# First stage of a hybrid mixer: queries and keys/values projected together, tile by tile

## The chip, the cores and the metric

The kernel runs on one core of a Trainium2 chip. The metric is the device time of one execution in microseconds, the median of the runs. A core has five engines with instruction streams of their own: TensorE (PE; PEld are its weight loads), VectorE (DVE), ScalarE (ACT), GpSimd (POOL) and SyncE (SP), which here only issues DMAs. ScalarE issues some DMAs too, in the same stream as its arithmetic. Each stream runs in order; semaphores tie them together.

## The reference, cut to what matters

The input x has 1024 tokens of 1024 features. It is layer-normed once, then passes through two layers. A layer projects all tokens to 3992 columns, feeds four groups of heads (A: banded attention, B: a chunked recurrence, C: a gated recurrence, D: attention over compressed, selected and recent keys), projects their outputs back and norms the sum.

```python
h = layer_norm(x, ln0_g, ln0_b)
for l in range(DEPTH):                                  # 2
    y = hybrid_mixer(h, w_in[l], b_in[l], ...)          # A, B, C, D from h @ w_in[l] + b_in[l]
    h = layer_norm(DN_ALPHA * h + y, ln_g[l], ln_b[l])
```

For group D, the columns `dq` (256) are queries, which are rotated by position; `dkv` (276) holds two keys, which are rotated too, two values, and the gates of D and B; `dx` (128) is compressed over windows of 32 tokens by a small two-layer network into some 63 keys and values. All are sums over the 1024 features of h.

## The kernel before

Tokens are worked on in halves of 512, that is four tiles of 128. A stage is one half in one layer, so there are four stages; stage 0 is the first half in layer 0. In each stage the groups come in the order D, C, A, B. A group first projects, then mixes; while one group mixes, tile by tile, the program already writes the projections of the next one in between, so that TensorE has matmuls to lie beside the softmax work.

Numbers are float32 in two parts: a weight or activation is rounded to the matmul's format (`hi`) and the rest (`lo`) is kept beside it. A product is three matmuls (hi hi, hi lo, lo hi). So each weight piece that comes from memory (`load_piece`, lines 270 to 280) costs a DMA on SyncE's queue into one of two raw buffers, a cast on ScalarE (L276) and a subtraction on GpSimd (L277), and then lies in one of six split buffers (tag `W`). `load_in` brings a chunk of columns as four pieces of two feature blocks each.

In stage 0, `bring(t)` (L542) norms a tile of x in place (`norm`, lines 188 to 213: statistics on VectorE, Ln and Exp on ScalarE, four short VectorE steps, then two passes over 1024 columns, L210 subtract mean and times gain, L211 times deviation and plus bias). `to_feature` (L258) then transposes it on TensorE, in two groups of four, with a cast (L266) and a subtraction (L267) per group. `proj_tok` (L287) projects tokens: per tile 24 matmuls, three for each of eight feature blocks. For `dq` its result gets its bias (L520) and is rotated on GpSimd in five steps (`rope`, L327). `proj_feat` (L305) projects with the features in the rows, 24 matmuls of 512 columns per 128 columns.

Group D in stage 0 goes: `dq` with `bring` for the four tiles, constants (`load_consts`: masks and tables, loaded and cast on GpSimd, L252), `dx`, its compression (lines 586 to 612), `dkv` with key rotation and transposes, then the mixing, whose first step is `front(0)`; its projection `dz` (48 matmuls of 512 columns) is written after that, but may run earlier. The one-hot rows (L554 to 556) that mark key blocks are written under the keys in stages 0 and 2, and are read in stages 1 and 3.

PSUM for projections and transposes is two banks (pool `pj`). The pool with tag `P` has six buffers of 1024 columns, used for gain and bias, one-hot rows, constants on their way, the compression weights, and later for scores.

The order within each engine's stream is not that of the code alone. A planner takes the instructions by readiness in a time model, earlier code first, and writes the streams; it also ties each DMA issue to an earlier one where too many would be open.

Of the kernel before, what the change touches and what calls it, by code (L numbers as in the profile page):

```python
# [10 lines left out]
F32 = mybir.dt.float32  # L11
F32R = mybir.dt.float32r
# [3 lines left out]
OP = mybir.AluOpType  # L16
# [3 lines left out]
T, D, DEPTH = 1024, 1024, 2  # L20
NT = T // 128
TH = T // 2
NTH = NT // 2
# [131 lines left out]
def tile_hybrid(ctx, tc, I, out, dbg=None, depth=DEPTH):  # L155
# [3 lines left out]
    def f(ap):  # L159
        return ap.bitcast(F32)  # L160
# [12 lines left out]
    def cload(name, shape, q=SY):  # L173
        t_ = const.tile(shape, F32, name=name + "_sb")
        q.dma_start(t_, I[name])
        return t_

    def row_bc(src):
        return bass.AP(tensor=src.tensor, offset=src.offset, ap=[[0, 128], [1, src.shape[-1]]])
# [2 lines left out]
    acc = fix.tile([128, NTH, D], F32, tag="acc", name="acc")  # L182
    SY.dma_start(acc[:, 0, :], I['x'][0:128, :])
    ident = cload('ident', [128, 128])
    S.preload_act_table_set("natural_log_exp_and_others")


    def norm(x_t, gb, spread=False, dst=None):
        st = sm.tile([128, 2, 6], F32, tag="st", name="st", bufs=2)
        for j in range(2):  # L190
            V.bn_stats(out=st[:, j, :], in_=x_t[:, j * 512:(j + 1) * 512])
        mv = sm.tile([128, 2], F32, tag="mv", name="mv", bufs=2)
        V.bn_aggr(out=mv, in_=st)
        ve = sm.tile([128, 4], F32, tag="ve", name="ve", bufs=2)
        V.tensor_scalar(ve[:, 0:1], mv[:, 1:2], LN_EPS, None, op0=OP.add)
        S.activation(out=ve[:, 1:2], in_=ve[:, 0:1], func=AF.Ln)
        S.activation(out=ve[:, 2:3], in_=ve[:, 1:2], func=AF.Exp, scale=-0.5)
        V.tensor_tensor(ve[:, 1:2], ve[:, 2:3], ve[:, 2:3], op=OP.mult)
        V.tensor_tensor(ve[:, 1:2], ve[:, 1:2], ve[:, 0:1], op=OP.mult)
        V.tensor_scalar(ve[:, 1:2], ve[:, 1:2], -0.5, 1.5, op0=OP.mult, op1=OP.add)  # L200
        V.tensor_tensor(ve[:, 3:4], ve[:, 1:2], ve[:, 2:3], op=OP.mult)
        if spread:
            V.scalar_tensor_tensor(ve[:, 0:1], mv[:, 0:1], -1.0, ve[:, 3:4], op0=OP.mult, op1=OP.mult)
            S.activation(out=x_t, in_=x_t, func=AF.Identity, scale=ve[:, 3:4], bias=ve[:, 0:1])
            V.tensor_tensor(x_t, x_t, gb[0], op=OP.mult)
            G.tensor_tensor(x_t, x_t, gb[1], op=OP.add)
            return
        for j in range(2 if dst is not None else 1):
            c_ = slice(j * 512, (j + 1) * 512) if dst is not None else slice(0, D)
            V.scalar_tensor_tensor(x_t[:, c_], x_t[:, c_], mv[:, 0:1], gb[0][:, c_], op0=OP.subtract, op1=OP.mult)  # L210
            V.scalar_tensor_tensor(x_t[:, c_], x_t[:, c_], ve[:, 3:4], gb[1][:, c_], op0=OP.mult, op1=OP.add)  # L211
            if dst is not None:
                (SY if j else S).dma_start(dst[:, c_], x_t[:, c_])

    def load_gb(g, b, tag=None):
        if tag is not None:
            gb2 = mp.tile([128, 2, D], F32, tag=tag, name="gb2")
            gb = [gb2[:, 0, :], gb2[:, 1, :]]
        else:
            gb = [mp.tile([128, D], F32, tag="P", name="gb", bufs=PB) for _ in range(2)]  # L220
        SY.dma_start(gb[0], row_bc(g))
        SY.dma_start(gb[1], row_bc(b))
        return gb

    gb0 = load_gb(I['ln0_g'], I['ln0_b'])
    for t in range(1, NTH):
        S.dma_start(acc[:, t, :], I['x'][t * 128:(t + 1) * 128, :])
    cos = cload('cos', [128, NT, 32], S)
# [16 lines left out]
    def load_consts():  # L245

        for name, dst in (('masks', masks), ('cmask', cmask), ('lvm', lvm), ('sel', sel)):
            d2 = dst.rearrange("p a b -> p (a b)") if len(dst.shape) == 3 else dst
            n = d2.shape[1]
            m_ = mp.tile([128, 1024], F32, tag="P", name="m_", bufs=PB)  # L250
            SY.dma_start(m_[:, :n], I[name] if len(I[name].shape) == 2 else I[name].rearrange("p a b -> p (a b)"))
            G.tensor_copy(d2, m_[:, :n])  # L252
        for name, dst in (('rowok', rowok), ('rope_e', rope_e), ('impk', impk), ('rowsel', rowsel)):
            SY.dma_start(dst, I[name])
# [32 lines left out]
    def proj_tok(l, ch, evac, before=None):  # L287
        n = len(CHUNKS[ch])
        W = load_in(l, ch)
        bias = wp.tile([128, 276], F32, tag="bias", name="bias", bufs=1)  # L290
        SY.dma_start(bias[:, :n], row_bc(I['b_row'][l, CH_OFF[ch]:CH_OFF[ch] + n]))
        for t in range(NTH):
            if before is not None:
                before(t)
            ps = pj.tile([128, 512], F32, tag="pj", name="ps_p")
            for k in range(8):
                a = hT['hi'][:, k, t * 128:(t + 1) * 128]
                b = hT['lo'][:, k, t * 128:(t + 1) * 128]
                hi, lo = W[k // 2][0][:, k % 2, :], W[k // 2][1][:, k % 2, :]
                PE.matmul(ps[:, :n], a, hi, start=(k == 0), stop=False)  # L300
                PE.matmul(ps[:, :n], a, lo, start=False, stop=False)  # L301
                PE.matmul(ps[:, :n], b, hi, start=False, stop=(k == 7))  # L302
            evac(t, ps[:, :n], bias)

    def proj_feat(l, ch, evac):  # L305
        n = len(CHUNKS[ch])
# [148 lines left out]
    def groups(stage):  # L455
# [61 lines left out]
        def ev_q(dst):  # L517
            def ev(t, ps, bias):
                qt = sm.tile([128, 4, 64], F32, tag="qt", name="qt")
                V.tensor_tensor(qt, ps.rearrange("p (h d) -> p h d", h=4), bias[:, :256].rearrange("p (h d) -> p h d", h=4),  # L520
                                op=OP.add)
                rope(dst[:, t, :].rearrange("p (h z d) -> p h z d", h=4, z=2), qt, 4, cos[:, T0 + t, :], sin[:, T0 + t, :],
                     twice=True)
            return ev

        def ev_kv(dst, Vt, extra=None, rest=None, T1=T0):
            def ev(t, ps, bias):
                kt = sm.tile([128, 2, 64], F32, tag="qt", name="kt")
                V.tensor_tensor(kt.rearrange("p a b -> p (a b)"), ps[:, 0:128], bias[:, 0:128], op=OP.add)
                V.tensor_tensor(Vt[:, T1 + t].rearrange("p a b -> p (a b)"), ps[:, 128:256], bias[:, 128:256], op=OP.add)  # L530
                if rest is not None:
                    V.tensor_tensor(rest[:, t, :], ps[:, 256:276], bias[:, 256:276], op=OP.add)
                kr = sm.tile([128, 2, 64], F32, tag="kr", name="kr")
                rope(kr, kt, 2, cos[:, T0 + t, :], sin[:, T0 + t, :])
                c_ = slice((T1 + t) * 128, (T1 + t + 1) * 128)
                stack_k(kr, dst[:, 0:2, c_], 128, 128, extra=None if extra is None else extra[0:64, c_])
            return ev

        def group_D():
            hT['hi'] = fix.tile([128, 8, TH], F32R, tag="hThi", name="hT_hi")  # L540
            hT['lo'] = fix.tile([128, 8, TH], F32R, tag="hTlo", name="hT_lo")
            def bring(t):  # L542
                if stage == 0:
                    h_t = acc[:, t, :]
                    norm(h_t, gb0)
                else:
                    h_t = mp.tile([128, D], F32, tag="P", name="h_t", bufs=PB)
                    SY.dma_start(h_t, hd[hf][t])
                to_feature(h_t, t)
            if hf == 0:  # L550
                lay['Vd'] = mp.tile([128, NT, 2, 64], F32, tag="Vd", name="Vd")
                lay['KD'] = mp.tile([128, 3, T], F32R, tag="KD", name="KD")
                for j in range(2):
                    oh = mp.tile([16, 512], F32, tag="P", name="oh", bufs=PB)  # L554
                    SY.dma_start(oh, I['onehot'][:, 512 * j:512 * j + 512])
                    G.tensor_copy(lay['KD'][64:80, 2, 512 * j:512 * j + 512], oh)
                lay['vc'] = sm.tile([64, 64], F32, tag="vc", name="vc")
                G.memset(lay['vc'], 0.0)
                lay['Kc'] = sm.tile([128, 1, 64], F32R, tag="Kc", name="Kc")
                lay['xtail'] = sm.tile([128, 16], F32, tag="xtail", name="xtail")  # L560
            Vd, KD, vc, Kc, xtail = (lay[k] for k in ('Vd', 'KD', 'vc', 'Kc', 'xtail'))
            qd = mp.tile([128, NTH, 512], F32, tag="q", name="qd")
            proj_tok(l, 'dq', ev_q(qd), bring)
            if stage == 0:
                load_consts()
            yield

            XT = mp.tile([128, 2, 544], F32, tag="ca", name="XT")
# [42 lines left out]
            rope(kc[:, 1:2, :], kc[:, 0:1, :], 1, rope_e[:, hf, 0:32], rope_e[:, hf, 32:64], P=32)  # L611
            stack_k(kc[:, 1:2, :], Kc[:, :, 32 * hf:32 * hf + 32], 32, 32)

            proj_tok(l, 'dkv', ev_kv(KD, Vd, KD[:, 2, :], gi))
            gs = sm.tile([128, NTH, NH, 3], F32, tag="gs", name="gs")
            gsv = gs.rearrange("p t a b -> p t (a b)")
            S.activation(out=gsv, in_=gi[:, :, 0:12], func=AF.Exp, scale=-1.0)
# [620 lines left out]
```

## Time and profile before

| | |
|---|---|
| three runs | 1589.19, 1591.62, 1594.03 us, median 1591.62 |
| profiled execution | 1595.7 us, span 1593.9 us |
| TensorE busy (share of the span) | 1471.4 us (92%) |
| weight loads | 1184.5 us (74%) |
| VectorE | 1054.0 us (66%) |
| GpSimd | 854.2 us (54%) |
| ScalarE | 791.5 us (50%) |
| mean granted clock of TensorE | 0.973 |

Times in rows are microseconds from the first instruction of the span; a row of a timeline gives the start and then the duration. Engine names with a small q (SPq, ACTq) are the issue of DMAs. An arrow in brackets names what ended the idle time in front of an instruction. Matmuls are pipelined, so the spacing of their starts, not their duration, is what each adds.

### The profile page before, as it was taken

The page shows a single profiled execution, that of the slowest core. Times are in us where ns is not written, and L with a number is a line of the kernel's source. Part 1 is how long each engine was busy: PE and PEld are TensorE (multiplying, and loading weights), DVE is VectorE, ACT ScalarE, POOL GpSimd, SP SyncE. Part 2 cuts the span into 40 slices and gives each one's busy share as a digit, 9 for nine tenths or more (in the row PEclk, how much of TensorE's full clock was granted, in tenths as well). Part 3 has the DMA queues.
Part 4 walks back from the last instruction along what each step waited for, and adds up shares of the span by engine and source line. Part 5 has one row for each costly group of instructions (what it writes and reads, how often), then busy time and mean ns, then how long its engine had stood idle before and what let it go on. Part 6 is the DMA issues. An engine that isn't in the chain of part 4 may idle for free.

```text
span 1593.9 us, 29097 instructions
## 1 busy us (share of the span) xinstructions
PE 1471.4 (92%) x10674; PEld 1184.5 (74%) x10674; DVE 1054.0 (66%) x2494; ACT 791.5 (50%) x1865; POOL 854.2 (54%) x1182
## 2 busy tenths in 40 slices
PE   3899999989979998999998999999997999899995
PEld 3787688768867766887886877887886876588684
DVE  6347755795597788348549568359449778844767
ACT  2357535444356765345535564445534576534551
POOL 3733685556653308844576348844575330784443
PEclk9999999999989999999999999999998999999997
DMA  5221123441352100224234311224125210032311
GB/s 189 74 76 53 28 57 98 148 147 53 110 164 57 53 1 15 74 70 148 67 87 149 96 53 28 74 70 150 51 82 173 76 54 1 2 78 63 106 53 53
DMA packets 64894, 126.93 MB, mean 80 GB/s; under 512 B 10256, under 2 KB 16176, under 8 KB 64752
## 3 DMA queue, kind: packets, MB, share of 16 engines
q1 hardware_dynamic: 63888, 122.99, 26.6%
q10 hardware_dynamic: 864, 2.10, 0.4%
q8 instruction: 84, 1.38, 0.4%
q14 instruction: 58, 0.48, 0.1%
HBM read 114.57 MB, written 10.49 MB: 78 GB/s over the span
## 4 chain that ended last, share of the span: by engine, by line
PE 56%; DVE 17%; POOL 13%; DMA 5%; issue 5%; ACT 3%; SPq 0%; DVEq 0%; POOLq 0%; ACTq 0%
PE ps_f L315 6%; PE ps_f L317 6%; PE ps_f L316 6%; PE ps_pt L442 4%; PE O L449 4%; PE ps_p L300 3%; DMA w_raw<-in_w_in 3%; PE ps_p L301 3%; PE ps_p L302 3%; POOL w_split L277 3%; PE S_ps L388 2%; PE ps_o L491 2%; PE ps_o L493 2%; DVE QK L970 2%; PE ps_o L492 2%
## 5 line engine op out<-in xcount | busy, mean ns | idle before, releaser
L277 POOL TENSOR_TENSOR w_split<-w_raw,w_split 128x512 fp32r<-128x512 f32 (+2 forms) x320 | 416.5, 1309 | 379.5 <-ACT w_split L276 356.3
L276 ACT CAST w_split<-w_raw 128x512 fp32r<-128x512 f32 (+2 forms) x320 | 194.5, 610 | 246.1 <-DMA w_raw<-in_w_in 136.3
L315 PE MATMUL ps_f<-hT_hi,w_split 128*128 128x512 f32 x608 | 244.9, 403 | 0.0
L316 PE MATMUL ps_f<-hT_lo,w_split 128*128 128x512 f32 x608 | 242.6, 399 | 0.0
L317 PE MATMUL ps_f<-hT_hi,w_split 128*128 128x512 f32 x608 | 241.6, 399 | 0.0
L300 PE MATMUL ps_p<-w_split,hT_hi 128*128 128x256 f32 (+1 forms) x768 | 227.4, 299 | 12.3 <-DVE hT_lo L267 8.6
L301 PE MATMUL ps_p<-w_split,hT_hi 128*128 128x256 f32 (+1 forms) x768 | 222.9, 291 | 0.3 <-POOL w_split L277 0.3
L302 PE MATMUL ps_p<-w_split,hT_lo 128*128 128x256 f32 (+1 forms) x768 | 222.1, 290 | 0.0
L407 ACT ACTIVATE P<-S_ps,stt 128x256 f32<-128x256 f32 (+3 forms) x256 | 133.3, 528 | 69.1 <-DVE stt L402 42.5
L300 PEld LDWEIGHTS ps_p<-w_split,hT_hi 128*128 128x128 f32 x768 | 150.3, 196 | 17.3 <-DVE hT_lo L267 10.3
L301 PEld LDWEIGHTS ps_p<-w_split,hT_hi 128*128 128x128 f32 x768 | 150.2, 196 | 3.8 <-issue 2.3
L302 PEld LDWEIGHTS ps_p<-w_split,hT_lo 128*128 128x128 f32 x768 | 149.9, 195 | 1.8 <-issue 1.2
L315 PEld LDWEIGHTS ps_f<-hT_hi,w_split 128*128 128x128 f32 x608 | 114.8, 189 | 26.8 <-issue 2.9
L317 PEld LDWEIGHTS ps_f<-hT_hi,w_split 128*128 128x128 f32 x608 | 114.7, 189 | 26.6 <-issue 0.8
L316 PEld LDWEIGHTS ps_f<-hT_lo,w_split 128*128 128x128 f32 x608 | 114.9, 189 | 23.9 <-issue 0.8
L402 DVE TENSOR_REDUCE stt<-S_ps 128x1 f32<-128x384 f32 (+3 forms) x182 | 110.0, 624 | 32.3 <-PE S_ps L400 11.1
L491 PE MATMUL ps_o<-w_split,Y 128*128 128x512 f32 x256 | 111.3, 435 | 10.7 <-DVE acc L498 6.5
L442 PE MATMUL ps_pt<-ident_sb,P 128*128 128x128 f32 x648 | 104.3, 289 | 8.8 <-DVE P L432 8.2
L493 PE MATMUL ps_o<-w_split,Y 128*128 128x512 f32 x256 | 104.6, 417 | 4.3 <-POOL Y L477 4.1
L442 PEld LDWEIGHTS ps_pt<-ident_sb,P 128*128 128x128 f32 x648 | 73.8, 145 | 46.3 <-issue 38.1
L492 PE MATMUL ps_o<-w_split,Y 128*128 128x512 f32 x256 | 103.7, 405 | 0.0
L449 PE MATMUL O<-PT,Vd 128*64 128x256 f32 x528 | 84.9, 411 | 6.1 <-DVE PT L447 6.0
(359 smaller groups left out, 3172.8 us busy)
## 6 DMA issues: line engine op xcount, KB each, us to landing
w_raw<-in_w_in SPq DMA_DIRECT2D x224, 256.0 KB, 2.7
w_raw<-in_w_out SPq DMA_DIRECT2D x64, 256.0 KB, 2.7
w_raw<-in_w_in SPq DMA_DIRECT2D x16, 276.0 KB, 2.8
w<-in_w SPq DMA_DIRECT2D x8, 512.0 KB, 5.5
hs<-acc SPq DMA_DIRECT2D x8, 512.0 KB, 2.6
h_t<-hs SPq DMA_DIRECT2D x8, 512.0 KB, 4.3
acc<-hs SPq DMA_DIRECT2D x8, 512.0 KB, 4.0
out<-acc SPq DMA_DIRECT2D x7, 512.0 KB, 2.7
```

The lines of the kernel that those rows point to most:

```text
L276: S.copy(out=hi, in_=raw_)
L277: G.tensor_tensor(lo, raw_, f(hi), op=OP.subtract)
L300: PE.matmul(ps[:, :n], a, hi, start=(k == 0), stop=False)
L301: PE.matmul(ps[:, :n], a, lo, start=False, stop=False)
L302: PE.matmul(ps[:, :n], b, hi, start=False, stop=(k == 7))
L315: PE.matmul(ps, a, x1, start=(k == 0), stop=False)
L316: PE.matmul(ps, a, x2, start=False, stop=False)
L317: PE.matmul(ps, b, x1, start=False, stop=(k == 7))
L442: PE.transpose(ps[:, h, :], P[c][h // 2][:, h % 2, kb * 128 - a:kb * 128 - a + 128], ident)
L449: PE.matmul(O[64 * g:64 * g + 64, :], Vt(k0 + kb, g), PT[:, 2 * g:2 * g + 2, :].rearrange("p a b -> p (a b)"), start=(first and kb == 0), ...
L491: PE.matmul(ps, a, hi, start=(k == 0), stop=False)
L493: PE.matmul(ps, b, hi, start=False, stop=(k == 1))
```

## The change

In stage 0 alone, `dq` and `dkv` are projected together. A new function `proj_first` takes each tile through `bring`, then through the 24 matmuls of `dq` and the 24 of `dkv`. The raw weights of `dq` are requested near the top, on SyncE's queue, into two buffers of tag `P`; their split form lies in the buffers `KQ` and `Y`, which other groups use later. Gain and bias of the first norm move to ScalarE's queue, ahead of the x tiles 1 to 3. The first tile's two passes are cut into halves of 512 columns. The one-hot rows are written after `dkv`, in stages 0 and 2, and the constants after `proj_first`. The arithmetic is the same.

```diff
-    def norm(x_t, gb, spread=False, dst=None):
+    def norm(x_t, gb, spread=False, dst=None, halves=False):
...
-        for j in range(2 if dst is not None else 1):
-            c_ = slice(j * 512, (j + 1) * 512) if dst is not None else slice(0, D)
+        halves = halves or dst is not None
+        for j in range(2 if halves else 1):
+            c_ = slice(j * 512, (j + 1) * 512) if halves else slice(0, D)
...
-        SY.dma_start(gb[0], row_bc(g))
-        SY.dma_start(gb[1], row_bc(b))
+        q.dma_start(gb[0], row_bc(g))
+        q.dma_start(gb[1], row_bc(b))
...
-    gb0 = load_gb(I['ln0_g'], I['ln0_b'])
+    gb0 = load_gb(I['ln0_g'], I['ln0_b'], q=S)
+    for j in range(2):
+        first_raw.append(mp.tile([128, 2, 512], F32, tag="P", name="w_raw0", bufs=PB))
+        for z in range(2):
+            o_ = 8 * CH_OFF['dq'] + (2 * j + z) * 512
+            SY.dma_start(first_raw[j][:, z, :], I['w_in'][0, :, o_:o_ + 512])
...
+    def proj_first(bring, ev_a, ev_b):
+        W = [[], load_in(0, 'dkv')]
+        for j, tag in enumerate(('KQ', 'Y')):
+            w = mp.tile([128, 2, 2, 512], F32R, tag=tag, name="w_first")
+            for z in range(2):
+                S.copy(out=w[:, z, 0], in_=first_raw[j][:, z, :])
+                G.tensor_tensor(w[:, z, 1], first_raw[j][:, z, :], f(w[:, z, 0]), op=OP.subtract)
+                W[0].append([w[:, z, v].rearrange("p (k n) -> p k n", k=2) for v in range(2)])
...
+        for t in range(NTH):
+            bring(t)
+            for W_, n, bias, ev in ((W[0], 256, ba, ev_a), (W[1], 276, bb, ev_b)):
+                ps = pj.tile([128, 512], F32, tag="pj", name="ps_p")
+                for k in range(8):
...
+                    PE.matmul(ps[:, :n], a, hi, start=(k == 0), stop=False)
+                    PE.matmul(ps[:, :n], a, lo, start=False, stop=False)
+                    PE.matmul(ps[:, :n], b, hi, start=False, stop=(k == 7))
+                ev(t, ps[:, :n], bias)
...
-                    norm(h_t, gb0)
+                    norm(h_t, gb0, halves=(t == 0))
...
+            def block_rows():
                 for j in range(2):
                     oh = mp.tile([16, 512], F32, tag="P", name="oh", bufs=PB)
...
-            proj_tok(l, 'dq', ev_q(qd), bring)
             if stage == 0:
+                proj_first(bring, ev_q(qd), ev_kv(KD, Vd, KD[:, 2, :], gi))
                 load_consts()
+            else:
+                proj_tok(l, 'dq', ev_q(qd), bring)
...
-            proj_tok(l, 'dkv', ev_kv(KD, Vd, KD[:, 2, :], gi))
+            if stage > 0:
+                proj_tok(l, 'dkv', ev_kv(KD, Vd, KD[:, 2, :], gi))
+            if hf == 0:
+                block_rows()
```

## Rows read from the trace of the kernel before

**Rows 1.** Stretches: engines' busy us (instructions), TensorE's granted clock, DMA share, GB/s.
```profile
0.00:18.10 18.10, 0.01 (x1) 0.01 (x1) 12.58 (x32) 3.27 (x7) 5.88 (x15) 1.00 0.81 265
18.10:38.70 20.60, 13.03 (x57) 11.94 (x58) 11.54 (x20) 4.82 (x12) 8.89 (x8) 1.00 0.43 133
38.70:50.10 11.40, 9.25 (x73) 8.41 (x73) 3.95 (x7) 3.16 (x6) 10.15 (x17) 1.00 0.05 14
50.10:75.50 25.40, 22.25 (x196) 19.82 (x195) 6.60 (x19) 8.18 (x17) 18.21 (x34) 1.00 0.33 94
...
95.00:1593.90 1498.90, 1409.53 (x10270) 1129.82 (x10268) 1013.07 (x2405) 762.90 (x1803) 799.24 (x1096) 0.97 0.26 77
```

**Rows 2.** Timeline of VectorE, the first norm: start, duration, instruction.
```profile
5.60 1.29 DVE L191 BATCH_NORM_STATS2 st<-acc 128x6 f32<-128x512 f32 x2 [4.64 <-DMA acc<-in_x]
...
15.80 4.45 DVE L211 SCALAR_TENSOR_TENSOR acc<-acc,ve,gb 128x1024 f32<-128x1024 f32 x2
```

**Rows 3.** Timeline of TensorE, 18 to 56 us.
```profile
18.09 1.97 PE L262 MATMUL ps_t<-ident_sb,acc 128*128 128x128 f32 x8 [18.09 <-DVE acc L211]
...
22.97 0.58 PE L300 MATMUL ps_p<-w_split,hT_hi 128*128 128x256 f32 x1 [2.92 <-DVE hT_lo L267]
...
41.83 0.66 PE L262 MATMUL ps_t<-ident_sb,acc 128*128 128x128 f32 x4 [1.40 <-DVE hT_lo L267]
42.25 0.36 PE L300 MATMUL ps_p<-w_split,hT_hi 128*128 128x256 f32 x1
...
45.18 1.39 PE L262 MATMUL ps_t<-ident_sb,acc 128*128 128x128 f32 x8
...
55.70 0.29 PE L300 MATMUL ps_p<-w_split,hT_hi 128*128 128x276 f32 x1
```

**Rows 4.** Timeline of ScalarE and its DMA issues, up to 29 us.
```profile
0.77 1.35 ACTq L227 DMA_DIRECT2D acc<-in_x  x3
...
5.82 0.33 ACTq L175 DMA_DIRECT2D sin_sb<-in_sin  x1
8.36 0.20 ACT L196 ACTIVATE ve<-ve 128x1 f32<-128x1 f32 x1 [6.34 <-DVE ve L195]
...
28.34 0.62 ACT L276 CAST w_split<-w_raw 128x512 fp32r<-128x512 f32 x1 [3.97 <-DMA w_raw<-in_w_in]
```

**Rows 5.** Raw weight pieces issued before 30 us: from issue to landing.
```profile
DMA to landing us min/median/max: 3.1/4.2/6.2
```

**Rows 6.** Stretches around the hole at 88.2 us, columns as in the first group.
```profile
88.20:90.20 2.00, 0.00 (x0) 0.00 (x0) 0.75 (x1) 1.15 (x2) 1.14 (x1) 0.95 0.48 131
90.20:93.40 3.20, 3.17 (x15) 3.18 (x16) 1.65 (x3) 2.94 (x7) 1.54 (x2) 0.50 0.32 82
```

**Rows 7.** The x tiles 1 to 3 (line 227): from issue to landing.
```profile
DMA to landing us min/median/max: 5.0/7.2/10.0
```

**Rows 8.** Gain and bias of the first norm: from issue to landing.
```profile
DMA to landing us min/median/max: 7.4/8.9/10.4
```

**Rows 9.** Groups by line and shape on GpSimd, 0 to 95 us: busy us, mean ns.
```profile
L277 POOL TENSOR_TENSOR w_split<-w_raw,w_split 128x512 fp32r<-128x512 f32 x14 | 18.8, 1355 | 14.4 <-ACT w_split L276 14.4
L277 POOL TENSOR_TENSOR w_split<-w_raw,w_split 128x552 fp32r<-128x552 f32 x4 | 5.5, 1380 | 1.9 <-ACT w_split L276 1.8
```

**Rows 10.** Timeline of GpSimd: a constant's cast; first and last rotation step of a tile.
```profile
19.12 1.50 POOL L252 CAST masks_r<-m__407 128x384 fp32r<-128x384 f32 x1
...
46.55 0.73 POOL L331 TENSOR_TENSOR rp<-qt,cos_sb 128x256 f32<-128x256 f32 x1
...
48.77 0.73 POOL L339 TENSOR_TENSOR qd<-rp,rp 128x256 f32<-128x256 f32 x1
```

**Rows 11.** Timeline of VectorE: first and last step of the compression's chain.
```profile
62.06 0.16 DVE L598 COPY hb<-Hps 128x1 f32<-128x1 f32 x1 [4.73 <-PE Hps L595]
...
70.89 0.18 DVE L350 TENSOR_TENSOR Kc<-ps_k,Kc 64x32 fp32r<-64x32 f32 x1 [1.61 <-ACT Kc L347]
```

**Rows 12.** The tile acc up to 40 us: durations in ns, shortest, median, longest.
```profile
L211 DVE SCALAR_TENSOR_TENSOR acc<-acc,ve,gb x4: 1281/1758/2297, 15.8 to 27.0; 128x1024 f32<-128x1024 f32 x4
```

## What the change will do to the time: the prediction

> **What bounds the kernel now.** The table above comes first: TensorE is the busiest engine by far, 92% of the span. A share over the whole span hides stages, so I cut it into pieces [rows 1]. From 95 us to the end TensorE is busy 1409.5 of 1498.9 us: there it is the bound, and 89.4 us of idle time are spread over the rest of the program. The start is another matter: nothing in 18.1 us, 13.0 of the next 20.6, 9.3 of 11.4, 22.3 of 25.4.
>
> Why it starts late is in the timeline of VectorE [rows 2]. Its first statistics begin when the first x tile has landed, at 5.6 us. The second gain-and-bias pass of that tile (L211) starts only at 15.8 us: VectorE did statistics and first passes of tiles that had landed meanwhile. Two such passes then take 4.45 us together, and the first transposes follow at 18.09 us [rows 3]. After that come holes although tiles are normed. ScalarE stands 3.97 us in front of a weight cast until 28.34 us [rows 4]; behind it in the same stream waits the cast of the transposed activations, and for that TensorE. That weight piece took 6.2 us to land [rows 5], and it could be requested only when an earlier one was split, since raw pieces have two buffers.
>
> TensorE also runs slowly here: the matmul at 22.97 us lasts 0.58, the one at 42.25 us 0.36 [rows 3]. At a granted clock of 0.50, its lower level, fifteen matmuls of 256 columns take 3.2 us, 0.213 each [rows 6]; from 42.25 to 45.18 us 24 of them pass, 0.122 each.
>
> I count to one mark: the moment when dq, dx, dkv and the compression matmuls are through, 75.5 us now. The work up to it at the fast clock: transposes 4 x 1.4 (the eight at 45.18 us), dq 4 x 2.93, dx 50.1 to 55.7 = 5.6, dkv 4 x 3.16 (2.93 x 276/256), and 4.0 for the compression and the key transposes (22.25 busy between 50.1 and 75.5, less 5.6 and 12.6) [rows 1, 3]. That is 5.6 + 11.7 + 5.6 + 12.6 + 4.0 = 39.5 us. So 36 us ahead of the mark are idle time or slow clock; that is what the change can reach.
>
> **The change part by part.**
>
> Loads. ScalarE's queue now brings x1, x2 and x3, issued from 0.77 us on, 0.45 apart; the quickest lands 5.0 us after its issue, the slowest 10.0, which puts them at 5.8, 8.4 and 11.7 us [rows 4, 7]. Gain and bias on SyncE's queue take 7.4 and 10.4 us [rows 8]. After the change gain, bias and x1 are the first three 512 KB on ScalarE's queue, so I give them the same landings: bias at 8.4, x1 at 11.7. The 1 MB of dq weights stands where gain and bias stood on SyncE's queue: in by about 12.5 us.
>
> The added wait. The sin table went out at 5.82 us, just after x1 had landed, though ScalarE had no work since its table load at 2 us [rows 4]. I read this as loads of both queues taking turns at eight slots, where the tenth waits for the second. With four more issues early on SyncE's queue, sin would be the fourteenth and wait for the sixth, x1: 11.7 us. Behind it in ScalarE's stream stand Ln and Exp of the first norm (8.36 us now) and the weight casts. Two ends: not held, the first transposes can start at about 9.8 us (bias 8.4, half a pass 0.7, 0.7 around it); held, Ln at 11.8, four short VectorE steps 1.2 in all with Exp, half a pass 0.7: 13.8 us. I take 13.8, since today's order has the table ahead of Ln. That is 4.3 us before 18.09.
>
> First tile. Normed in halves, its first four transposes (1.0 us at the slow clock), the ScalarE cast (0.6) and the VectorE subtraction (0.7) lead to the first dq matmul at about 16.2 us, now 22.97. 24 x 0.213 = 5.1 end at 21.3 us. GpSimd can have the four dq pieces split by 12.6 + 4 x 1.36 = 18.0 us [rows 9]; no piece waits for a buffer, as all four have room.
>
> dkv weights. Four splits of 1.38 us [rows 9] follow; two end at 20.8 us. The other two need the same two raw buffers, free at 19.4 and 20.8: then a load, a cast of 0.65 and the split. The load takes 3.1 to 6.2 us [rows 5]; I take 3.1, because what landed beside the long one, 1 MB of compression weights, has no buffer this early after the change. The last piece is ready near 26, the first tile's dkv ends at 26.5 us; with the long load at 29.6. TensorE has the second tile's transposes and dq (1.4 + 2.9 to 5.1) to lie beside this.
>
> Remaining tiles. dkv of the second, 3.2, and two tiles of 1.4 + 2.93 + 3.16 = 7.5: 18.2 us. Where tiles meet, transposes wait 1.40 us for the casts [rows 3]; three times: 4.2. This makes 26.5 + 18.2 + 4.2 = 49 us. VectorE's norms (three more tiles of about 7 us from 14.6 on) end near 36, ahead of their use. GpSimd's rotation is 2.95 us per tile for the queries (46.55 to 49.50) [rows 10] and half of that for the keys, 4.5 against 7.5 of TensorE. It hides there; with a split in front of it a PSUM bank is held 1.4 us longer, which is the price where the cover goes.
>
> Then dx 5.6 and the 4.0: 58.6 us, against 75.5. That is 17 us less.
>
> What is late next. From the compression's first result to the stacked compressed keys it is 62.06 to 71.07 us, 9.0 us of short steps that pass between engines [rows 11], now covered by dkv matmuls. After the change only dz is left, 48 matmuls of 0.232 (5.57 / 24) = 11.1 us, and the compression matmuls, some 2.5 of the 4.0; to be covered are the 9.0, those 2.5 and about 1.9 for moving XT (three steps like the 0.62 cast [rows 4]): 13.4 wanted, 13.6 there. No slack, so I charge one hole like that at 88.2 us: 2.0 idle and, after it, 3.2 us at granted clock 0.50, which costs 1.6 [rows 6]. Less what fits: 3 us. Its bounds are 0 and 12.7, the latter if dz comes after the chain because its weights are not split in time: 11.1 and the clock's 1.6.
>
> Moved at no cost. The four constant casts, the first 1.50 us [rows 10], I take at 6 us together. GpSimd's work up to the mark is 10.9 of splits, 18 of rotation, 2.7 for dx (half width), 6 of casts, and two one-hot casts of no more than 1.5 each: 41 of some 46 us from 12.6 on. It fits; if it does not, up to 6 us of casts come in front of the first scores. The one-hot rows are read in the second half of the tokens alone, so no instruction waits for their later place, here or in the third stage. Two more half passes cost VectorE some 0.3 us, off the path.
>
> Sum: 17 - 3 = 14 us. The profiled execution took 1595.7, so 1581.7; the median of the runs shown, 1591.6, is 4.1 below it, so the time is 1578.
>
> One row speaks against splits beside norms: L211 takes 1.28 us at its shortest and 2.30 at its longest [rows 12]; the long ones are the pair at 15.8 us, beside two splits. If the eight splits (10.9) and the passes of three tiles (6 x 1.28 = 7.7) took turns from 12.6 us on, the last split would end at 31 instead of 26, 5 us later. The Trainium skill (page SBUF — State Buffer, section SBUF: two separate sides) has a VectorE instruction with two SBUF inputs and a GpSimd one that reads SBUF exclude each other for a whole instruction. By that rule the 5 us would be lost in full, a time of 1583; the row agrees in kind, but TensorE's other work can lie beside part of it.
>
> **The rivals.**
>
> 1. GpSimd sets the pace: splits take turns with the norms (up to 5), and the long load (3.1). Gain 14 - 7 = 7, so 1585. For it: the L211 row. Against it: the second tile's dq is there to do meanwhile.
>
> 2. The start is quicker, but the gain turns into a hole: dz does not cover the compression chain, 12.7 charged instead of 3. Gain 4 or less, 1587 to 1593. For it: no slack in the cover. Against it: two weight buffers are free for dz while dx runs.
>
> 3. ScalarE's stream is not held by sin (4 us more) and the chain is covered (3 more): 1571.
>
> 4. Slower. The planner lays out all later work anew. Each added hole like that at 88.2 us costs 2.0 + 1.6 = 3.6 us [rows 6], beside the 89.4 us idle now behind 95 us. To be slower by 0.3% it takes 14 + 4.8 = 19 us, from the sixth such hole on: 1600. Against it: the later program is unchanged but for the one-hot rows.
>
> That the change does not do what it says (dq and dkv still far apart because dkv weights come late) is the far end of 1.
>
> **How the numbers follow.** Forecast (1573 to 1583) 0.55; rival 3 (below 1573) 0.08; rival 1 (1583 to 1587) 0.15; rival 2 0.12; rival 4 0.10. A measurement of this kernel tells about 0.3%, 4.8 us, from no change. Faster: 0.55 + 0.08 + 0.15 = 0.78; same 0.12; slower 0.10. The range from 1566 to 1593 leaves out rival 4 and a little below.
>
> **What would show it.** First transposes near 14 us (10 if ScalarE is not held); the sin table just after x1; the first dq matmul near 16; dkv of the first tile before dq of the third; dx from about 49 us; the mark near 58. It is wrong if dx starts after 59, if TensorE idles over 6 us between dx and the first scores, or if its idle time behind the first scores differs from 89 us by more than 8.

## The result, and the profile after

The changed kernel takes 1600.7 us (median of 7 runs), the kernel before 1591.6 (7 runs beside them): a ratio of 1.0055, 95% interval [1.0041, 1.0069]. By the ratio it is slower by 8.8 us, where 14 us less were forecast. The profiled executions, 1597.7 and 1595.7 us, lie only 2.0 apart, the one being the shortest of its kernel's runs and the other above all of its own. So I read stages and single waits here, not the two ends.

Stages of the changed kernel, columns as in [rows 1]:

```profile
0.00:18.10 18.10, 1.51 (x7) 1.52 (x8) 9.31 (x21) 3.79 (x8) 4.95 (x14) 1.00 0.89 315
18.10:38.70 20.60, 10.28 (x54) 8.74 (x53) 19.15 (x34) 6.32 (x16) 17.15 (x17) 0.81 0.49 145
38.70:50.10 11.40, 9.40 (x65) 8.72 (x64) 2.33 (x8) 1.01 (x3) 6.26 (x13) 0.90 0.10 25
50.10:75.50 25.40, 24.16 (x150) 21.68 (x149) 6.68 (x18) 7.91 (x17) 15.55 (x32) 0.93 0.17 47
...
95.00:1595.90 1500.90, 1407.92 (x10287) 1128.95 (x10286) 1013.43 (x2406) 763.33 (x1805) 799.19 (x1096) 0.98 0.26 77
```

The first tile comes 1.5 us earlier, and then the second stretch is worse than before: TensorE works 10.3 us in it instead of 13.0, while VectorE (19.15 of 20.6) and GpSimd (17.15) are busy nearly all the time. The clock column (0.81, before 1.00) can't be compared there. In the kernel before it shows 1.00, yet the matmuls of dq lie 0.21 us apart up to 38.7 us, which is the spacing that goes with 0.50 in [rows 6]:

```profile
33.12 0.41 PE L301 MATMUL ps_p<-w_split,hT_hi 128*128 128x256 f32 x1
33.33 0.41 PE L302 MATMUL ps_p<-w_split,hT_lo 128*128 128x256 f32 x1
```

In all these traces the recorded changes of the clock begin only after TensorE's first matmuls (at 38.8 us before, at 23.9 us after, where the spacing falls from 0.21 to 0.12 us), and the column counts the time ahead of them as 1.00. Behind 95 us 93.0 us of TensorE's idle time remain, 3.6 more than before.

Timeline of TensorE after, the places that answer to [rows 3]:

```profile
16.59 1.97 PE L269 MATMUL ps_t<-ident_sb,acc 128*128 128x128 f32 x8 [16.59 <-DMA bias_a<-in_b_row]
20.29 0.58 PE L333 MATMUL ps_p<-w_first,hT_hi 128*128 128x256 f32 x1 [1.74 <-DVE hT_lo L274]
...
24.82 0.29 PE L333 MATMUL ps_p<-w_split,hT_hi 128*128 128x276 f32 x1
...
29.17 0.63 PE L269 MATMUL ps_t<-ident_sb,acc 128*128 128x128 f32 x4 [2.66 <-DVE acc L213]
31.38 0.60 PE L333 MATMUL ps_p<-w_split,hT_hi 128*128 128x276 f32 x1 [1.57 <-ACT w_split L283]
33.08 1.12 PE L269 MATMUL ps_t<-ident_sb,acc 128*128 128x128 f32 x4 [1.10 <-DVE hT_lo L274]
37.45 0.58 PE L333 MATMUL ps_p<-w_first,hT_hi 128*128 128x256 f32 x1 [3.25 <-DVE hT_lo L274]
...
91.58 0.58 PE L307 MATMUL ps_p<-w_split,hT_hi 128*128 128x256 f32 x1 [3.83 <-DVE Zd L544]
...
100.13 0.42 PE L421 MATMUL S_ps<-KD,A 128*128 128x128 f32 x2
```

(The transposes read no bias_a; what they need is the first half pass, which VectorE ends at 16.53.) The second tile's dq starts at 37.45 us. From 26.4 on, when the half of the first tile's dkv for which weights were there had run, TensorE got only eight transposes and one matmul. The matmuls of dx start at 66.5 (50.1 before), the first scores at 100.1 (94.6 before).

VectorE after, in its order, answering to [rows 2, 12]:

```profile
11.84 1.22 DVE L199 TENSOR_TENSOR ve<-ve 128x1 f32<-128x1 f32 x1 [2.92 <-ACT ve L198]
13.09 1.19 DVE L200 TENSOR_TENSOR ve<-ve 128x1 f32<-128x1 f32 x1
14.31 0.15 DVE L201 TENSOR_SCALAR ve<-ve 128x1 f32<-128x1 f32 x1
14.38 1.28 DVE L192 BATCH_NORM_STATS2 st<-acc 128x6 f32<-128x512 f32 x2
...
24.23 1.56 DVE L212 SCALAR_TENSOR_TENSOR acc<-acc,mv,gb 128x1024 f32<-128x1024 f32 x1
...
25.78 1.51 DVE L212 SCALAR_TENSOR_TENSOR acc<-acc,mv,gb 128x1024 f32<-128x1024 f32 x1
...
27.75 1.28 DVE L213 SCALAR_TENSOR_TENSOR acc<-acc,ve,gb 128x1024 f32<-128x1024 f32 x1
...
30.08 1.44 DVE L213 SCALAR_TENSOR_TENSOR acc<-acc,ve,gb 128x1024 f32<-128x1024 f32 x1
31.44 0.98 DVE L199 TENSOR_TENSOR ve<-ve 128x1 f32<-128x1 f32 x1
32.35 0.68 DVE L274 TENSOR_TENSOR hT_lo<-ps_t,hT_hi 128x512 fp32r<-128x512 f32 x1
...
35.08 1.71 DVE L213 SCALAR_TENSOR_TENSOR acc<-acc,ve,gb 128x1024 f32<-128x1024 f32 x1
36.71 0.68 DVE L274 TENSOR_TENSOR hT_lo<-ps_t,hT_hi 128x512 fp32r<-128x512 f32 x1
```

GpSimd and ScalarE after, beside that:

```profile
11.78 3.71 POOL L319 TENSOR_TENSOR w_first<-w_raw,w_first 128x512 fp32r<-128x512 f32 x3 [5.25 <-ACT w_first L318]
...
30.39 2.03 POOL L259 CAST sel_sb<-m__602 128x1024 fp32r<-128x1024 f32 x1
32.38 2.65 POOL L284 TENSOR_TENSOR w_split<-w_raw,w_split 128x552 fp32r<-128x552 f32 x2
```

```profile
10.61 0.33 ACTq L175 DMA_DIRECT2D sin_sb<-in_sin  x1
10.99 0.20 ACT L197 ACTIVATE ve<-ve 128x1 f32<-128x1 f32 x1 [8.97 <-DMA acc<-in_x]
...
29.86 0.20 ACT L197 ACTIVATE ve<-ve 128x1 f32<-128x1 f32 x1 [5.07 <-DVE ve L196]
...
30.21 0.57 ACT L273 CAST hT_hi<-ps_t 128x512 fp32r<-128x512 f32 x1
30.67 1.21 ACT L283 CAST w_split<-w_raw 128x552 fp32r<-128x552 f32 x2
```

Two things are to be seen. A step on one element per partition, L199 and L200, takes 1.2 us while GpSimd subtracts, and L201, which has one tensor operand, 0.15. The Trainium skill (page SBUF — State Buffer, section SBUF: two separate sides) has such two-input instructions and GpSimd's reads of SBUF exclude each other; this trace agrees: the two steps end at 13.06 and 14.28 us, the first two of the three subtractions (1.24 us each) at 13.04 and 14.26, and L201 runs beside the third. So even the shortest step pays the length of the other engine's instruction. And VectorE's stream has the first passes of tiles 3 and 4 (24.23, 25.78) ahead of the second pass of tile 2 (27.75), and second passes of tiles 3 and 4 (30.08, 35.08) ahead of tile 2's two subtractions (32.35, 36.71), for which TensorE waits.

### The profile page after: what moved, and what is told of

It reads as the page before. It is cut to its first block, busy times and chain, and to the rows that moved or that the text cites. A ratio compares the mean times of both kernels' runs of the same rounds, so it can differ in the third digit from the quotient of the medians.

```text
span 1595.9 us, 29101 instructions
## 1 busy us (share of the span) xinstructions
PE 1468.1 (92%) x10674; PEld 1181.9 (74%) x10674; DVE 1056.3 (66%) x2496; ACT 790.9 (50%) x1865; POOL 853.9 (54%) x1182
## 4 chain that ended last, share of the span: by engine, by line
PE 62%; DVE 18%; POOL 9%; issue 4%; DMA 4%; ACT 3%; SPq 0%; ACTq 0%; DVEq 0%; POOLq 0%
PE ps_f L348 6%; PE ps_f L349 6%; PE ps_f L350 6%; PE ps_pt L475 4%; PE ps_p L307 4%; PE O L482 4%; PE ps_p L308 4%; PE ps_p L309 4%; DMA w_raw<-in_w_in 2%; PE S_ps L421 2%; PE ps_o L524 2%; PE ps_o L526 2%; POOL w_split L284 2%; PE ps_o L525 2%; DVE QK L1009 2%
## 5 line engine op out<-in xcount | busy, mean ns | idle before, releaser
L284 POOL TENSOR_TENSOR w_split<-w_raw,w_split 128x512 fp32r<-128x512 f32 (+2 forms) x316 | 410.7, 1307 | 360.1 <-ACT w_split L283 345.4
L307 PE MATMUL ps_p<-w_split,hT_hi 128*128 128x256 f32 (+1 forms) x704 | 206.1, 295 | 7.7 <-DVE Zd L544 3.8
L308 PE MATMUL ps_p<-w_split,hT_hi 128*128 128x256 f32 (+1 forms) x704 | 202.1, 289 | 0.0
L309 PE MATMUL ps_p<-w_split,hT_lo 128*128 128x256 f32 (+1 forms) x704 | 201.8, 288 | 0.0
L307 PEld LDWEIGHTS ps_p<-w_split,hT_hi 128*128 128x128 f32 x704 | 135.8, 194 | 11.2 <-DVE hT_lo L274 4.3
L308 PEld LDWEIGHTS ps_p<-w_split,hT_hi 128*128 128x128 f32 x704 | 135.9, 193 | 2.8 <-issue 1.9
L309 PEld LDWEIGHTS ps_p<-w_split,hT_lo 128*128 128x128 f32 x704 | 135.6, 193 | 2.1 <-issue 1.5
L349 PEld LDWEIGHTS ps_f<-hT_lo,w_split 128*128 128x128 f32 x608 | 114.8, 189 | 23.9 <-issue 0.8
```

The costliest lines, as they stand in the source:

```text
L284: G.tensor_tensor(lo, raw_, f(hi), op=OP.subtract)
L349: PE.matmul(ps, a, x2, start=False, stop=False)
```

## The experiments

Ratios are to the kernel before, run beside each. "At 150 us" is how much later TensorE was than in the kernel before: the median shift of matching matmuls that start there at 150 to 175 us, from one profiled execution each. The kernels that fuse run some of these matmuls in another order, so single shifts scatter by several us about their median.

| kernel | ratio [95%] | dx starts | first scores | at 150 us |
|---|---|---|---|---|
| before | 1 | 50.1 | 94.6 | 0 |
| changed | 1.0055 [1.0041, 1.0069] | 66.5 | 100.1 | +6.8 |
| e1 no splits | 1.0013 [0.9996, 1.0030] | 59.8 | 93.0 | -0.4 |
| e2 norms in order | 1.0022 [1.0010, 1.0035] | 64.8 | 98.5 | +5.2 |
| e3 not fused | 1.0013 [1.0001, 1.0026] | 48.0 | 88.2 | -6.4 |
| e4 fused only | 1.0027 [1.0013, 1.0041] | 64.4 | 97.8 | +4.4 |
| f1 not fused, in order, halves, one-hot back | 1.0024 [1.0010, 1.0038] | 48.9 | 89.2 | -5.4 |
| f2 changed, one-hot back | 1.0045 [1.0031, 1.0059] | 66.7 | 100.1 | +6.7 |
| f3 before, no norm | 0.9988 [0.9973, 1.0003] | 44.0 | 86.1 | -7.9 |
| f4 not fused, one-hot back | 0.9993 [0.9979, 1.0008] | 47.6 | 89.1 | -5.5 |
| g1 no splits, in order | 0.9996 [0.9982, 1.0009] | 57.0 | 91.0 | -2.4 |
| g2 two tiles fused, one-hot back | 1.0036 [1.0023, 1.0049] | 61.9 | 97.7 | +3.1 |
| g3 f4 with 16 matmuls more | 1.0000 [0.9988, 1.0013] | 47.5 | 88.9 | -5.8 |
| i1 splits on VectorE, in order, one-hot back | 1.0008 [0.9996, 1.0020] | 60.8 | 95.2 | +1.8 |
| i2 f4, dq splits on VectorE | 0.9995 [0.9976, 1.0013] | 49.8 | 89.7 | -4.9 |

**e1, no splits.** It leaves out the subtractions of the first stage's dq and dkv weights. `load_piece` got the same edit for dkv:

```diff
-                G.tensor_tensor(w[:, z, 1], first_raw[j][:, z, :], f(w[:, z, 0]), op=OP.subtract)
+                G.memset(f(w[:, z, 1]), 0.0)
```

> Leaves out part of the computation: the subtractions that make the lo half of the first stage's dq and dkv weights; that half is filled with zeros on GpSimd before x has landed (TensorE still runs every matmul). VectorE's and TensorE's order stay nearly as in the changed kernel. Theory A (GpSimd's eight splits, 10.9 us, stretch VectorE's short steps and delay the dkv pieces): the two short steps of 1.2 us at 12 us fall to 0.2, first dq matmul near 18 instead of 20.3, the second tile's dq near 32 instead of 37.5, dx near 60 instead of 66.5, time 1594. Theory B (the order in VectorE's stream, norms of tiles 3 and 4 ahead of tile 2's casts, does it): the short steps fall too, but the second tile's dq stays at 34 or later and dx at 63 or later, time 1598 to 1601.

Theory A's numbers came: the second dq at 32.6, dx at 59.8. VectorE in e1, the same two steps as at 11.84 and 13.09 above:

```profile
11.95 0.16 DVE L199 TENSOR_TENSOR ve<-ve 128x1 f32<-128x1 f32 x1 [3.17 <-ACT ve L198]
12.15 0.16 DVE L200 TENSOR_TENSOR ve<-ve 128x1 f32<-128x1 f32 x1
```

The first scores are 7.2 us earlier, the time 6.7 us lower. The first transposes start 2.0 us earlier (14.62 instead of 16.59).

**e2, norms in order.**

```diff
+        if behind is not None:                  # acc[:, t - 1, D - 1:D], the last of the tile before
+            V.tensor_copy(mv[:, 0:1], behind)
         V.bn_aggr(out=mv, in_=st)
```

> VectorE's order mended by one short copy per tile: the statistics of a tile are closed only when the tile before it is normed, so no pass of a later tile stands ahead of an earlier one. GpSimd's work is unchanged. Theory B (order): second tile normed near 25 us instead of 29, its dq near 29 instead of 37.5, dx near 58 instead of 66.5, time 1593. Theory A (GpSimd beside it): second dq at 34 or later, dx at 63 or later, time 1598 to 1601.

Order alone does less for the start than theory B said: second dq at 34.9, first scores 1.6 us earlier. The time fell by 5.3 us all the same (the intervals do not meet), more than its start accounts for.

**e3, e4: the halves of the change.** e3 leaves dkv out of `proj_first` and projects it after the compression; e4 has `load_gb` on SyncE's queue, no halves, and requests `first_raw` inside `proj_first`.

> The fusion alone undone: dq tile by tile from the early weights, with gain and bias on ScalarE's queue, halves and late constants as in the changed kernel; dkv projected after the compression as before. Theory C (the fusion costs: 8 instead of 4 splits by 35 us, and no dkv left to cover the compression chain): dx at 50 or earlier, no hole behind 85 us, time 1588 to 1592. Theory D (early loads and the new order in VectorE's stream cost by themselves): dx later than 52 us, time 1595 to 1600.

> The fusion alone done: gain and bias on SyncE's queue, dq weights requested after the first x tile, ident, gain and bias, no halves. Theory C: first transposes near 18 us as before the change, dkv of the first tile still late (after 40 us), dx near 65, hole behind 85 us, time 1600 to 1604. Theory D: dx near 60, time 1594 or less.

The starts are as theory C has them: without fusion dx at 48.0 and no hole, with it dx at 64.4 and a wait of 3.84 us for Zd. The times are as neither has them. e3 is 6.4 us ahead at 150 us and ends 2 us behind. And e4, with the old loads, is faster than the whole change by 4.5 us (the intervals touch), though its first transposes start 3.3 us later, at 19.88: its second tile's dq is earlier, at 35.6, and its first scores too. Beside the fusion, the early loads bring nothing.

**f1 to f4: what an earlier start is worth, and the one-hot rows.** f1 is e3 with the edit of e2, halves for all tiles and the rows back. f3 drops the call of `norm` from the kernel before. f2 (f4 likewise, on e3) puts the rows back:

```diff
+            if stage == 2:
+                block_rows()
             Vd, KD, vc, Kc, xtail = (lay[k] for k in ('Vd', 'KD', 'vc', 'Kc', 'xtail'))
```

> Fusion undone, early loads kept, all four tiles normed in halves and one after the other, one-hot rows where they were before the change. If the start is worth what it gains (theory E): second tile's transposes near 25 us instead of 29, dx near 44 instead of 50, TensorE 8 us ahead of the kernel before at 150 us and no hole of 2.4 us at 750, time 1584 to 1587. If a stretch behind it takes the gain back (theory F: at 185 to 210 us GpSimd is busy all the time, TensorE has holes there and its granted clock falls to 0.5 behind them): 8 us ahead at 150 us, 3 or less at 230, time 1590 to 1593.

> The changed kernel with one edit undone: the one-hot rows of the third stage stand in front of its dq again; the first stage is as changed. TensorE waits 2.44 us for P near 750 us in all kernels with the rows moved, 0.21 in the one before. If the move does it: that wait is 0.3 or less and the time 2 us below the changed kernel, 1598 to 1599. If the wait comes from elsewhere: still 2.4, and 1600 to 1601.

> The kernel before, and the first layer norm of the first half left out (x is transposed as it is): part of the computation is missing. It asks what an earlier start is worth. First transposes near 6 us, dq bound by its weights, dx near 40 instead of 50. Theory E (kept to the end): TensorE 10 us ahead at 150 us and still 8 or more at 1000, time 1583 to 1585. Theory F (taken back at 185 to 210 us): ahead by 3 or less behind it, time 1589 to 1593.

> Fusion undone, early loads kept as in the changed kernel (halves for the first tile alone, norms in the planner's order), one-hot rows where they were before the change. Differs from the kernel with the fusion alone undone only by the one-hot rows. If their move costs 2 us near 750: wait there 0.3 or less, time 1592 to 1594 (ratio to before 1.000), 2 us below that kernel. If not: the same as that kernel, ratio 1.0013.

TensorE's wait near 750 us, first in the changed kernel, then in f2:

```profile
752.60 1.08 PE L482 MATMUL Oa<-PT,Va 128*64 128x256 f32 x8 [2.44 <-DVE PT L480]
```

```profile
750.17 1.08 PE L482 MATMUL Oa<-PT,Va 128*64 128x256 f32 x8 [0.21 <-DVE PT L480]
```

The move of the rows in the third stage makes that wait: it is gone in all kernels with the rows back. In time it is 1.6 us (f2) and 3.2 us (f4 against e3); the intervals overlap, but both point to about 2 us.

Theory E fails. f3 is 7.9 us ahead at 150 us and in its one trace still 8.0 at the end (one of its shorter runs beside a long one of the kernel before), but the median of its 12 runs is 1.9 us below the kernel before, which cannot be told from none. f1 leads by 5.4 and comes out 3.8 us slower; f4, with the same lead, 1.1 us faster, which cannot be told from none either.

**g1, g2, g3.** g1 is e1 and e2 together. g2 fuses dkv for tiles 1 and 2 alone:

```diff
-            for W_, n, bias, ev in ((W[0], 256, ba, ev_a), (W[1], 276, bb, ev_b)):
+            for W_, n, bias, ev in ((W[0], 256, ba, ev_a), (W[1], 276, bb, ev_b))[:2 if t < 2 else 1]:
...
+            proj_tok(l, 'dkv', ev_kv(KD, Vd, KD[:, 2, :], gi), tiles=range(2 if stage == 0 else 0, NTH))
```

g3 adds to f4, in the last tile's `values` of the first stage:

```diff
+                for _ in range(16 if kb == 2 else 0):
+                    PE.matmul(O[0:64, :], zw, hT['hi'][:, 0, 0:256], start=False, stop=False)   # zw = 0
```

> Leaves out the lo half of the first stage's dq and dkv weights (zeros, no subtraction on GpSimd) and has the norms one after the other by a short copy per tile. Each of the two alone moved the first scores from 100.1 us to about 93 and 98.5. If the two causes (GpSimd's splits beside VectorE, VectorE's order) add up: second tile's dq at 29 or earlier, dx at 56 or earlier, first scores near 90, time 1592 to 1594. If they are one cause (the order only hurts because the steps are stretched): as without the splits alone, second dq 32.6, first scores 93, time 1595 to 1596. In both, a wait of 3.8 us for Zd stays, as nothing else is there to do.

> dq of all four tiles and dkv of the first two together; dkv of the last two after the compression, with its weights loaded and split a second time (5.5 us more on GpSimd); one-hot rows of the third stage where they were. If the compression chain lacks cover in the changed kernel (3.83 us wait for Zd and slow clock behind it): that wait and the slow clock go, dx 6 us earlier (60), first scores near 96 instead of 100, time 1594 to 1596. If not: first scores at 100 or later, time 1598 to 1600, as with the one-hot rows alone put back.

> The kernel without fusion, with early loads and the one-hot rows in their old place, and 16 more matmuls of 256 columns that add zeros, where TensorE waits 2.07 us for P at 187 us; behind that wait its granted clock is 0.5 for some 18 us in all three traces of this family, and the 5.5 us gained at 150 us become 2. If the wait brings the clock down and that takes the gain back: clock 0.9 or more from 188 to 208, 5 us ahead of the kernel before at 230 us, time 1587 to 1588 (ratio 0.997 or less). If GpSimd's stretch sets the time there: 2 to 3 us ahead at 230 in spite of the clock, time 1590 to 1592. If the clock falls all the same: no change.

g1: the second dq starts at 30.1, first scores at 91.0, 9.2 us earlier than in the changed kernel, where the two edits alone gave 7.2 and 1.6. At the start they add up; in time the two alone gave 6.7 and 5.3 us, together 9.4 us below the changed kernel. That is the time of the kernel before: splits and order together account for the loss, as far as leaving the splits out can say, for it takes away their work as well as their place beside VectorE.

g2: no wait for Zd is left, and the first scores are 2.4 us earlier than in f2; 1.4 us of it shows in the time, within the intervals. In its profiled run, its longest, the clock is near 0.50 from 620 to 640 us, where no other trace is below 0.83, and TensorE falls back by 5 us there.

g3: stretches of f4, then of g3, columns as in [rows 1]:

```profile
180.00:188.00 8.00, 6.47 (x116) 4.32 (x108) 6.53 (x16) 3.11 (x5) 8.00 (x19) 1.00 0.01 3
188.00:192.00 4.00, 3.35 (x38) 1.89 (x38) 3.96 (x12) 1.72 (x3) 4.00 (x10) 0.82 0.00 0
192.00:196.00 4.00, 4.00 (x44) 3.45 (x44) 3.93 (x12) 2.02 (x4) 4.00 (x9) 0.50 0.01 4
196.00:200.00 4.00, 4.00 (x54) 2.99 (x54) 3.15 (x13) 1.32 (x2) 4.00 (x8) 0.50 0.00 0
200.00:204.00 4.00, 4.00 (x53) 3.43 (x51) 2.69 (x8) 0.61 (x3) 2.75 (x7) 0.50 0.02 4
204.00:208.00 4.00, 4.00 (x16) 2.77 (x17) 3.40 (x10) 2.79 (x6) 2.36 (x2) 0.55 0.00 0
```

```profile
180.00:188.00 8.00, 7.89 (x115) 5.88 (x108) 6.53 (x15) 2.69 (x4) 8.00 (x18) 1.00 0.01 3
188.00:192.00 4.00, 2.78 (x58) 2.08 (x56) 3.93 (x12) 1.55 (x3) 4.00 (x10) 1.00 0.02 4
192.00:196.00 4.00, 2.25 (x53) 1.56 (x53) 3.97 (x10) 2.02 (x4) 4.00 (x9) 1.00 0.00 0
196.00:200.00 4.00, 4.00 (x46) 3.34 (x45) 4.00 (x15) 1.94 (x5) 3.86 (x7) 0.63 0.00 0
200.00:204.00 4.00, 4.00 (x15) 2.75 (x16) 3.00 (x8) 2.47 (x5) 4.00 (x8) 0.51 0.01 4
204.00:208.00 4.00, 4.00 (x53) 3.48 (x50) 3.97 (x12) 1.73 (x4) 1.74 (x2) 1.00 0.48 131
```

With the wait at 187 us filled (0.18 us instead of 2.07) the clock holds to 196 and is back at 204, and TensorE leads by 4.4 us at 200 to 225 us where f4 leads by 2.0. So the fall of the clock does take 2 to 3 us of the lead there. But the time of g3, ratio 1.0000, is no lower than f4's; where the rest of the lead goes these runs do not show.

**i1, i2: the same subtractions on VectorE.**

```diff
-                G.tensor_tensor(w[:, z, 1], first_raw[j][:, z, :], f(w[:, z, 0]), op=OP.subtract)
+                V.tensor_tensor(w[:, z, 1], first_raw[j][:, z, :], f(w[:, z, 0]), op=OP.subtract)
```

> The changed kernel, complete in what it computes, with the eight subtractions of the first stage's dq and dkv weights on VectorE instead of GpSimd, norms one after the other, one-hot rows as before the change. If it is GpSimd beside VectorE that costs (a subtraction of 552 columns takes 1.36 us there): short steps of VectorE back at 0.15 to 0.25 us, second tile's dq near 33, dx near 60, first scores near 94, time 1591 to 1594 (ratio 1.000). If it is the work of the splits wherever it is done: second dq at 36 or later, first scores at 98 or later, time 1597 or more.

> The kernel without fusion, early loads, one-hot rows as before the change, and the four dq subtractions on VectorE instead of GpSimd. If GpSimd beside VectorE costs there too: second tile's transposes before 28 instead of 29.4, dx at 45 or earlier, TensorE 7 us or more ahead of the kernel before at 150 us, time 1588 to 1590. If the order in VectorE's stream sets the second tile: as without this edit, 5.5 us ahead, time 1590 to 1592. In both the clock behind 187 us takes about 4 us back.

VectorE in i1, a subtraction and the next short step:

```profile
11.66 0.69 DVE L321 TENSOR_TENSOR w_first<-w_raw,w_first 128x512 fp32r<-128x512 f32 x1 [2.94 <-ACT w_first L320]
12.27 0.15 DVE L201 TENSOR_TENSOR ve<-ve 128x1 f32<-128x1 f32 x1
```

i1 computes all that the changed kernel does and is 7.5 us faster than it, the same as the kernel before within what can be measured. What the place of the subtractions does in it is read against e2 and g1, in order too: first scores at 98.5 with them on GpSimd, 95.2 on VectorE, 91.0 without. So of 7.5 us some 3.3 are the two engines beside each other and 4.2 the work wherever it is done; the second dq, at 36.6, is as late as the rival had it. In time i1 is 2.2 us below e2, no more than the one-hot rows are worth. So that the two engines hold each other up is shown in the steps and at the first scores; a gain in time from moving the subtractions is not shown. i2 shows no gain over f4; its first transposes, behind the subtractions, start at 19.9 instead of 16.8.

## Why the prediction was wrong

The step that failed is an overlap, in "dkv weights": "TensorE has the second tile's transposes and dq (1.4 + 2.9 to 5.1) to lie beside this", until 26.5 us. Its ground is in "Remaining tiles": "VectorE's norms (three more tiles of about 7 us from 14.6 on) end near 36, ahead of their use". What the runs showed in its place: the second dq starts at 37.45 us, behind the last weight piece (35.0) and not beside it, for two reasons.

The norm is late. The last pass did end at 36.8. But 7 us per tile, one after the other, would have had tile 2 normed near 21.6; it was normed at 29.0. VectorE worked on tiles 2, 3 and 4 in turns, and its steps were stretched beside the splits. I had seen the first in the trace before ("VectorE did statistics and first passes of tiles that had landed meanwhile") and had a row for the second (L211), and the forecast counts neither. The runs part the two: tile 2 is normed at 27.7 with the order mended (e2), at 25.4 without the splits (e1), at 22.5 with both (g1). So the splits beside the norms, which the forecast put at nothing and rival 1 at up to 5 us, weigh more than the order.

A bank is held. From tile 2 normed to its dq another 8.4 us pass, and 7.2, 7.3 and 7.6 in e1, e2 and g1, where splits or order or both are mended. In e3, without the fusion, tile 2 is normed no earlier than in the changed kernel (28.9), its eight transposes go in a row, and its dq starts 3.1 us behind the norm:

```profile
29.05 1.94 PE L269 MATMUL ps_t<-ident_sb,acc 128*128 128x128 f32 x8 [3.75 <-DVE ve L201]
31.97 0.58 PE L331 MATMUL ps_p<-w_first,hT_hi 128*128 128x256 f32 x1 [0.98 <-DVE hT_lo L274]
```

In the changed kernel the first tile's dkv, half done at 26.4, still holds one of the two PSUM banks of `pj`. The two groups of transposes take turns in the other, the second (33.08) waiting until VectorE has read out the first, and dq gets that bank when the second is read out, at 37.4. The prediction did not count these banks. That the bank is what holds dq is read from the waits and from the program; no run gives a third bank.

So TensorE had nothing to lie beside the late pieces, waited from 26 to 37 us, and ran the second dq at the lower clock at first (0.21 us per matmul up to 40.8). Counted as in the prediction, with 5.6 us for dx and 4.0 for the compression behind 66.5, the mark is at 76.1 us, against 75.5 before: a gain of 17 us became a loss of 0.6.

Point by point:

- The sin table holds ScalarE's stream: right (sent at 10.61, Ln at 10.99; 11.7 and 11.8 forecast).
- First transposes 13.8: 16.59. Four short steps with Exp, put at 1.2 us, took 4.2 (11.61 to 15.8): two stretched by the splits, and two statistics (1.28) in between. The first dq matmul, put at 16.2, followed at 20.29.
- Last dkv piece ready near 26: 35.0. Its cast on ScalarE (30.67) stood behind Ln of tile 4 and a cast for tile 2, both waiting for VectorE and TensorE, and GpSimd had the cast of sel (2.03) in front. The splits were priced by GpSimd's time, the other streams they hang on were not. The piece was of no use at once: in TensorE's stream the rest of that dkv stands behind the second dq, at 41.95.
- Rival 1 had the splits beside the norms, at 7 us: up to 5 for them and 3.1 for a long load. The load was short (3.0 and 3.5 us for the last two pieces), and without the splits the first scores come 7.2 us earlier (e1). So that its 7 agrees is luck, and I had set it against a gain that was not there.
- The compression chain, charged 3: between the mark and the first scores 24.0 us pass, 19.1 before, so 4.9. The wait for Zd [rows 6] grew to 3.83, with one of 0.8 ahead of it and the clock at 0.50 behind. The bounds held; rival 2's mechanism came without the gain.
- One-hot rows "at no cost", as no instruction waits for them: wrong in the third stage, about 2 us. Their move changed the order of later work near 750 us.
- Rival 4, six new holes behind 95 us: no; 3.6 us more idle time there. The sign came from the start.

0.6 + 4.9 = 5.5 us at the first scores and the 2 us near 750 make 7.5 of the 8.8, but this sum is not shown. In the two profiled executions the changed kernel is 6.8 us behind at 150 us and 3.1 at 200 to 225, so a late start is made up in part as an early one is lost. What stands without it are the times: with the splits out and the order mended the loss is gone (g1).

A start as forecast is not likely to have brought 14 us either: six kernels that lead by 4.9 to 7.9 us at 150 us come out between 1.9 us faster and 3.8 us slower. Part of the lead goes when the clock falls behind 187 us (f4, g3). The rest is open. None of the complete versions beats the kernel before by more than can be measured; f4 (0.9993) is the nearest.

## What to carry to other kernels

Where GpSimd subtracts or casts beside VectorE, price each VectorE step with two SBUF inputs, the shortest too, at the length of GpSimd's instruction. Take the finish of the second tile, not of all tiles, from the order in which an engine's stream really takes them. Before work is said to lie beside a wait, count the PSUM banks that half-done sums hold meanwhile. Before a start is shortened, leave its work out once and time that: it shows what the start is worth at the end.

## What the runs showed of the hardware

The granted clock can stay at 0.50 though TensorE works without a gap: in f4 from 192 to 204 us and some 2 us on either side, behind a wait of 2.07 us. The changed kernel waits 1.80 us at 187 and again later there, and its clock stays at 1.00.

TensorE time lost to the clock, span x (1 - mean granted clock) of a run, goes with the run's time: over 121 runs of the kernel before 0.42 us of time per us lost (correlation 0.70). The mean is 42.5 us there, 48.5 in the changed kernel, 53.1 in f4 and 55.9 in e3. Between kernels these means can't be set against each other as they stand: the kernel before has no record of its clock ahead of 38.8 us, when TensorE worked at the lower level, and f4 and e3 have theirs from 26.7 and 24.5 on. Behind 150 us, where the leads were measured, one trace each shows 42.0 us lost in the kernel before, 48.6 in f4 and 52.2 in e3. At 0.42 the 6.6 and 10.2 us more are an estimated 2.8 and 4.3 us, a part of the 4.4 and 8.5 us by which the two leads shrank. f3 lost 36.9 there, less than the kernel before, and its lead shrank too: the clock alone is not the cause.

GpSimd's own rows are stretched as well: the cast of sel takes 2.03 us in the changed kernel, with VectorE's passes beside it, and 1.04 in i1.
